# Two parts of the activations as one moving operand, and blocks of 256 columns

## The chip, the core and the metric

The kernel runs on one core of a Trainium2 chip. What counts is the device time of one execution in microseconds, as the median of the runs.

## What is computed

One decoder block for 256 tokens of width 2048, all in float32:

```python
h = rmsnorm(x, norm_w)
proj = h @ w_in          # z | x, B, C | dt | q | k | v | g_attn | g_merge
y = ssd_scan(silu(causal_dwconv(xBC)), softplus(dt + dt_bias), A)   # 64 heads in 8 groups
y_ssm = group_rmsnorm((y + D_skip * xs) * silu(z)) @ w_ssm_proj
y_attn = (attention(q, k, v) * silu(g_attn)) @ w_attn_proj          # 16 heads, causal
mixed = sigmoid(g_ssm + b) * y_ssm + sigmoid(g_att + b) * y_attn
out = rmsnorm(x + mixed @ w_out, final_norm_w)
```

With 256 tokens and blocks of 256, the block-sparse attention is plain causal attention of one block. The products with `w_in`, `w_ssm_proj`, `w_attn_proj` and `w_out` are nearly all of the work.

## The kernel before, in words

**Precision.** Each weight and each activation of the large products is split into an upper part and the rest (`hi`, `lo`), both of type float32r. A product is made of three matmuls: upper weights by upper activations, upper by lower, and lower by upper.

**The stream.** `stream()` (L46) lists blocks of weight columns in the order in which they are multiplied; a block is usually 512 columns wide with all 2048 rows, `sp` blocks have 1024 rows, `bc` blocks 256 columns. `chunks()` (L94) cuts each block into chunks of 128 partitions by 1024 values (512 KB), 480 in all; a chunk of a 512-column block holds two k tiles of 128 rows. The order is two `z` blocks, then eight groups of `bc`, `x`, `z` for the SSD branch (with gates `gs` and the projections `sp` between them), then `q`, `k`, `v`, `ga` four times for the attention, gates `gt` and projections `ap`, and `wo` at the end.

**The weight pipeline.** The loop over chunks stands at L801. In turn n it issues the load of chunk n + PF (L218; six buffers of `raw`, so a load waits until the chunk six before it is split), the upper part of chunk n + 4 on ScalarE (`split_hi`, L230; five buffers), the lower part of chunk n + 3 on VectorE (`split_lo`, L237; four buffers), one step of the tasks that take finished blocks out of PSUM (`evac`), the matmuls of chunk n, and a step of the SSD and attention tasks. These tasks are generators: each `yield` ends a step, and so the order of the instructions on each engine is written out by hand.

**The matmuls.** `matmuls` (L252, the instruction at L263) has two forms. Blocks `v` and `wo` have the activations as the stationary operand and 512 weight columns moving. All others, here called by-channel, have a strip of 128 weight columns stationary and the 256 tokens moving: three matmuls of 256 columns for each k tile and strip, into one of the four strips of an accumulator of 4 KB (two banks); there are two accumulators, `acc`, and four further banks for the small products. In the first two blocks the activations are those of `hp_hi`, `hp_lo`, not yet normalised; in `sp` and `ap` blocks they are named `ahi`, `alo` in the trace, elsewhere `h_hi`, `h_lo`.

**What follows a block.** `z_task`, `gate_task`, `sp_task`, `qkv_task`, `ap_task` read the whole accumulator once, on ScalarE or VectorE. `bc_task` and `x_task` make the causal convolution straight from PSUM, three VectorE operations to a step (L455). `ssd_task` does one group of the scan: transposes `px`, decays `e` (L524, L527, L531), products `yp` (L542), norm `pn`, and the two parts of the result for the `sp` blocks. Before block 15 a step of it is taken in every turn, later only in turns without an evacuation step, unless tasks pile up.

Of the kernel before, what the change touches and what calls it, by code (L numbers as in the profile page):

```python
# [24 lines left out]
# Chunks that loads and splits run ahead of the products.  # L25
PF, LA = 8, 3
# [19 lines left out]
def stream():  # L46
    """The weight stream: blocks (name, index, matrix, column pieces, first row, contraction rows)."""
# [4 lines left out]

    def sp(part, j):
        out.append(("sp", (part, j), "w_ssm_proj", [(j * 512, 512)], part * QR, QR))

    def gate(name, j):
        proj(name, j, ((C_GS if name == "gs" else C_GT) + j * 512, 512))

    for g in (0, 1):
        proj("z", g, (C_Z + g * 512, 512))  # L60
    for g in range(NG):
        proj("bc", g, (C_B + g * P, P), (C_C + g * P, P))
        proj("x", g, (C_X + g * 512, 512))
        if 1 < g + 1 < NG:
            proj("z", g + 1, (C_Z + (g + 1) * 512, 512))
        if g + 1 == NG:
            gate("gs", 0)
        if g > 2:
            part, half = divmod(g - 3, 2)
            sp(part, 2 * half)  # L70
            sp(part, 2 * half + 1)
# [9 lines left out]
    for u in range(4):  # L81
        for n, c in (("q", C_Q), ("k", C_K), ("v", C_V), ("ga", C_GA)):
            proj(n, u, (c + u * 512, 512))
    for j0 in (0, 2):
        for j in (j0, j0 + 1):
            gate("gt", j)
        for j in (j0, j0 + 1):
            out.append(("ap", j, "w_attn_proj", [(j * 512, 512)], 0, D))
# [5 lines left out]
def chunks():  # L94
    """(block number, first k tile, k tiles, columns) of each chunk of the stream."""
    out = []
    for b, (_, _, _, pieces, _, rows) in enumerate(stream()):
        cols = sum(n for _, n in pieces)
        per = CH // cols
        out += [(b, k, per, cols) for k in range(0, rows // P, per)]  # L100
    return out
# [16 lines left out]
def hybrid_block(  # L118
# [23 lines left out]
    def big(name, tag, dtype=F32):  # L142
        """4 KB of each partition; the tags are shared by what is not alive at the same time."""
# [36 lines left out]
    # The tensor engine's clock comes up while the first loads are under way.  # L180
# [3 lines left out]
    # mask[s, l]: s tile 0 against l 0..255, then s tile 1 against l 128..255.  # L184
# [7 lines left out]
    # amask[q, k]: q tile 0 against k 0..127, then q tile 1 against k 0..255.  # L192
# [11 lines left out]
    h_hi = hpool.tile([P, KT, S], F32R, name="h_hi")  # L204
    h_lo = hpool.tile([P, KT, S], F32R, name="h_lo")

# [1 line left out]
    raws, his, los = {}, {}, {}  # L208

    def halves(n):  # L210
        """The first chunk goes in two pieces, for an early start."""
        return (slice(0, CH),) if n else (slice(0, CH // 2), slice(CH // 2, CH))

    def load(n):
        if n < NCK:
            raws[n] = wpool.tile([P, CH], F32, tag="raw", name="raw", bufs=6)
            for h in halves(n):
                nc.sync.dma_start(raws[n][:, h], wpk[n][:, h])  # L218

    def part(n, which, bufs):  # L220
        """A part of chunk n; the last block's first half lies apart, as that block is gone through twice."""
        if NCK - 8 <= n < NCK - 4:
            return apool.tile([P, CH], F32R, tag="a" + which, name="a" + which)
        return wpool.tile([P, CH], F32R, tag="w" + which, name="w" + which, bufs=bufs)

    def split_hi(n):
        if n < NCK:
            his[n] = part(n, "hi", LA + 2)
# [3 lines left out]
    def split_lo(n):  # L232
        if n < NCK:
            los[n] = part(n, "lo", LA + 1)
# [5 lines left out]
    xt, hp_hi, hp_lo = [], [], []  # L240
    y_hi, y_lo = {}, {}
    o_hi, o_lo = {}, {}
    m_hi, m_lo = {}, {}

    def operand(name, k, sl=slice(0, S)):
        """(hi, lo) of k tile k of what the block multiplies."""
        for of, hi, lo in (("first", hp_hi, hp_lo), ("sp", y_hi, y_lo), ("ap", o_hi, o_lo), ("wo", m_hi, m_lo)):
            if name == of:
                return hi[k // 4][:, k % 4, sl], lo[k // 4][:, k % 4, sl]
        return h_hi[:, k, sl], h_lo[:, k, sl]  # L250

    def matmuls(n, acc, spans=((0, 0, 512), (1, 0, 512)), keep=False):  # L252
        b, k0, per, ncol = cks[n]
        name, i, _, _, row, rows = blocks[b]
        name = "first" if b < 2 else name
        last_k = rows // P - 1
        wh = his[n].rearrange("p (k c) -> p k c", k=per)
        wl = los[n].rearrange("p (k c) -> p k c", k=per)
        if not keep:
            del his[n], los[n]  # L260

        def mm(dst, a, bb, start, stop):
            nc.tensor.matmul(dst, a, bb, start=start, stop=stop, skip_group_check=True)  # L263

        if name in ("v", "wo"):
            for t, c0, c1 in spans:
                at = 0 if keep else t * 512
                dst = acc[:, at : at + c1 - c0]
                for i in range(per):
                    k = k0 + i  # L270
                    ah, al = operand(name, row // P + k, slice(t * P, (t + 1) * P))
                    mm(dst, ah, wh[:, i, c0:c1], k == 0, False)
                    mm(dst, ah, wl[:, i, c0:c1], False, False)
                    mm(dst, al, wh[:, i, c0:c1], False, k == last_k)
        else:
            for i in range(per):
                k = k0 + i
                ah, al = operand(name, row // P + k)
                for c in range(ncol // P):
                    dst = acc[:, c * S : (c + 1) * S]  # L280
                    cs = slice(c * P, (c + 1) * P)
                    mm(dst, wh[:, i, cs], ah, k == 0 and c % 2 == 0, False)
                    mm(dst, wh[:, i, cs], al, False, False)
                    mm(dst, wl[:, i, cs], ah, False, k == last_k)

# [1 line left out]
    for i in range(4):  # L287
        xt.append(big("xt", "xs" if i < 2 else "cumb"))
        hp_hi.append(apool.tile([P, 4, S], F32R, tag="ahi", name="hp_hi"))
        hp_lo.append(apool.tile([P, 4, S], F32R, tag="alo", name="hp_lo"))  # L290
    mpool = ctx.enter_context(tc.tile_pool(name="mpool", bufs=1))
    for n in range(8):
        ks = slice(n % 2 * 2, n % 2 * 2 + 2)
        nc.sync.dma_start(xt[n // 2][:, ks], xT[:, 2 * n : 2 * n + 2])
        if n < 6:
# [3 lines left out]
    for n in range(6, PF):  # L299
# [4 lines left out]
    def first_hi(n):  # L304
        if n < 8:
            for k in (2 * n, 2 * n + 1):
                nc.scalar.activation(
                    hp_hi[k // 4][:, k % 4], xt[k // 4][:, k % 4], AF.Identity, scale=nw[:, k : k + 1]
# [13 lines left out]
    def first_lo(n):  # L322
        if n < 8:
            for k in (2 * n, 2 * n + 1):
                nc.vector.scalar_tensor_tensor(
                    hp_lo[k // 4][:, k % 4], xt[k // 4][:, k % 4], nw[:, k : k + 1],
                    hp_hi[k // 4][:, k % 4].bitcast(F32), op0=OP.mult, op1=OP.subtract,
# [6 lines left out]
    def init_task():  # L334
        """The norm's factor of each token, along the free axis; h = h' * factor in its two parts."""
# [14 lines left out]
        for i in range(4):  # L350
# [6 lines left out]
            nc.scalar.copy(h_hi[:, ks], xt[i])  # L357
            yield
            nc.vector.tensor_sub(h_lo[:, ks], xt[i], h_hi[:, ks].bitcast(F32))
# [13 lines left out]
    def step(queue, heads=None):  # L373
        """One step of the first tasks of a queue; whether there was one."""
# [10 lines left out]
    scratch = dpool.tile([HEADS, S], F32, name="scratch")  # L385

    def dt_task(pd):
# [10 lines left out]
        # The two halves of the sum over k, transposed and added.  # L398
# [11 lines left out]
        # softplus(t) = max(t, 0) + log1p(exp(-|t|)); log1p(e) = 2 atanh(e / (2 + e))  # L410
# [35 lines left out]
    def tap(dst, u, ct):  # L446
        """Causal depthwise conv over the tokens (free axis): the token itself, then those before it."""
        nc.scalar.activation(dst, u, AF.Identity, bias=cb[:, ct : ct + 1], scale=cw[:, ct, 3:4])  # L448

    def conv(jobs):  # L450
        """The other taps of tiles (dst, u, ct), two tiles in turn, three operations a step."""
        ops = [(i + j, d) for i in range(0, len(jobs), 2) for d in (1, 2, 3) for j in range(2)]
        for at, (i, d) in enumerate(ops):
# [3 lines left out]
            )  # L457
            if at % 3 == 2:
                yield

    def bc_task(g, acc):
        bc = pool.tile([P, 2, S], F32, tag="bc", name="bc")
        jobs = [(bc[:, i], acc[:, i * S : (i + 1) * S], 32 + 8 * i + g) for i in range(2)]
# [14 lines left out]
    def x_task(g, acc):  # L478
        xs = big("xs", "xs")
        jobs = [(xs[:, i], acc[:, i * S : (i + 1) * S], 4 * g + i) for i in range(4)]  # L480
# [3 lines left out]
        ssd.append(ssd_task(g, xs))  # L484

    def ssd_task(g, xs):
# [118 lines left out]
        hi = apool.tile([P, 4, S], F32R, tag="ahi", name="ahi")  # L605
        lo = apool.tile([P, 4, S], F32R, tag="alo", name="alo")
        nc.scalar.copy(hi, y)
        yield
        nc.vector.tensor_sub(lo, y, hi.bitcast(F32))  # L609
        y_hi[g], y_lo[g] = hi, lo  # L610

# [1 line left out]
    SC = 128.0 ** -0.5  # L613

    def head_task(u, h, q, k, v, og):
# [30 lines left out]
        # k tile 0 against q 0..255, then k tile 1 against q 128..255  # L646
# [6 lines left out]
        if h == 3:  # L653
            yield
            hi = apool.tile([P, 4, S], F32R, tag="ahi", name="ahi")
            lo = apool.tile([P, 4, S], F32R, tag="alo", name="alo")
            nc.scalar.copy(hi, og)
            yield
            nc.vector.tensor_sub(lo, og, hi.bitcast(F32))
            o_hi[u], o_lo[u] = hi, lo  # L660

# [4 lines left out]
    def z_task(g, acc):  # L666
        t = big("z", "z")
        if g < 2:
            while "rsb" not in wk:
                yield  # L670
            nc.vector.tensor_tensor(
                t, acc.rearrange("p (a b) -> p a b", a=4),
                rsb.rearrange("p (o b) -> p o b", o=1).broadcast_to([P, 4, S]), op=OP.mult,
            )
            nc.scalar.activation(t, t, AF.Silu)
# [214 lines left out]
```

## Time and profile before

| | us |
|---|---|
| median of 3 runs (1467.83 to 1468.21) | 1467.96 |
| span of the profiled execution | 1466.1 |
| TensorE busy | 1454.4 (99%) |
| VectorE busy | 894.6 (61%) |
| ScalarE busy | 744.8 (51%) |
| mean DMA rate | 184 GB/s |

TensorE's row of busy time counts matmuls that overlap one another: the end of each is modelled, so the distance from one start to the next tells more than the length of one. Of the waits of the other engines, those for TensorE are time in which they had nothing to do.

### The profile page before, as it was taken

How to read it: one execution, taken by the hardware profiler on the slowest of the kernel's cores; microseconds unless marked ns; L12 is line 12 of the kernel's file. 1: busy time of each engine (PE TensorE's matmuls, PEld its weight loads, DVE VectorE, ACT ScalarE, POOL GpSimd, SP SyncE). 2: the span in 40 equal slices, each digit the busy share in tenths (PEclk: the TensorE clock that was granted, in tenths of full speed). 3: DMA queues.
4: the chain of work that ended last, by engine and by line, in shares of the span. 5: the costliest groups of instructions: out<-in, count | busy, mean ns of one | idle time of the engine just before them, and what ended most of it. 6: DMA issues, size and time to landing. Idle time of an engine off the chain costs nothing.

```text
span 1466.1 us, 27149 instructions
## 1 busy us (share of the span) xinstructions
PE 1454.4 (99%) x11410; PEld 1409.0 (96%) x11410; DVE 894.6 (61%) x1215; ACT 744.8 (51%) x870; POOL 5.3 (0%) x15
## 2 busy tenths in 40 slices
PE   9999999999999999999999999999999999999997
PEld 8999999999999999999999989999899999999886
DVE  7778777675667676866645455455454554545564
ACT  7545747564654565564544345445454454444452
POOL 0000000000000000000000000000000000000000
PEclk9999999999999999999999999999999999999999
DMA  8555656565565665665666565555655655666762
GB/s 326 164 170 190 206 163 202 158 208 180 176 191 179 181 193 163 198 209 165 177 184 186 180 187 166 176 173 165 192 160 173 187 158 175 185 185 177 267 211 80
DMA packets 74923, 269.99 MB, mean 184 GB/s; under 512 B 8304, under 2 KB 8624, under 8 KB 74416
## 3 DMA queue, kind: packets, MB, share of 16 engines
q1 hardware_dynamic: 74224, 267.49, 59.2%
q8 instruction: 89, 1.46, 0.4%
q10 hardware_dynamic: 576, 0.77, 0.2%
q14 instruction: 34, 0.28, 0.1%
HBM read 266.06 MB, written 2.16 MB: 183 GB/s over the span
## 4 chain that ended last, share of the span: by engine, by line
PE 98%; ACT 1%; DMA 0%; DVE 0%; issue 0%; SPq 0%; DVEq 0%
PE acc L263 93%; PE yp L542 2%; PE half L263 1%; PE px L502 0%; PE po L647 0%; PE ps L621 0%; DMA raw<-wpk 0%; PE pp L639 0%; PE pd L362 0%; PE ps L620 0%; PE po L648 0%; PE pcb L471 0%; PE pn L595 0%; ACT whi L230 0%; PE pcb L472 0%; ACT L684 0%
## 5 line engine op out<-in xcount | busy, mean ns | idle before, releaser
L237 DVE TENSOR_TENSOR wlo<-raw,whi 128x1024 fp32r<-128x1024 f32 (+1 forms) x477 | 582.2, 1222 | 492.2 <-PE acc L263 382.3
L230 ACT CAST whi<-raw 128x1024 fp32r<-128x1024 f32 (+1 forms) x477 | 497.4, 1048 | 559.9 <-PE acc L263 488.4
L263 PE MATMUL acc<-h_hi,whi 128*128 128x256 f32 x2432 | 697.0, 287 | 0.0
L263 PE MATMUL acc<-h_hi,wlo 128*128 128x256 f32 x2432 | 688.0, 283 | 0.0
L263 PE MATMUL acc<-h_lo,whi 128*128 128x256 f32 x2432 | 688.0, 283 | 0.0
L263 PEld LDWEIGHTS acc<-h_hi,whi 128*128 128x128 f32 x2432 | 466.3, 192 | 3.8 <-issue 3.0
L263 PEld LDWEIGHTS acc<-h_lo,whi 128*128 128x128 f32 x2432 | 466.6, 192 | 0.7
L263 PEld LDWEIGHTS acc<-h_hi,wlo 128*128 128x128 f32 x2432 | 466.3, 192 | 0.0
L263 PE MATMUL acc<-ahi,whi 128*128 128x256 f32 x768 | 218.7, 285 | 0.0
L263 PE MATMUL acc<-alo,whi 128*128 128x256 f32 x768 | 217.4, 283 | 0.2 <-DVE alo L609 0.2
L263 PE MATMUL acc<-ahi,wlo 128*128 128x256 f32 x768 | 217.3, 283 | 0.0
L263 PEld LDWEIGHTS acc<-ahi,whi 128*128 128x128 f32 x768 | 147.3, 192 | 0.9 <-issue 0.9
L263 PEld LDWEIGHTS acc<-alo,whi 128*128 128x128 f32 x768 | 147.4, 192 | 0.5 <-DVE alo L609 0.4
L263 PEld LDWEIGHTS acc<-ahi,wlo 128*128 128x128 f32 x768 | 147.4, 192 | 0.0
L263 PE MATMUL acc<-whi,h_hi 128*128 128x512 f32 x128 | 49.8, 389 | 0.0
L263 PE MATMUL acc<-wlo,h_hi 128*128 128x512 f32 x128 | 49.8, 389 | 0.0
L527 ACT ACTIVATE e<-e 128x768 f32<-128x768 f32 x32 | 27.1, 847 | 44.7 <-DVE e L524 44.6
L263 PE MATMUL acc<-whi,h_lo 128*128 128x512 f32 x128 | 49.8, 389 | 0.0
L455 DVE SCALAR_TENSOR_TENSOR xs<-acc,colt,xs 128x255 f32<-128x255 f32 (+2 forms) x96 | 40.2, 476 | 13.3 <-ACT xs L448 13.3
L263 PE MATMUL acc<-wlo,m_hi 128*128 128x512 f32 x104 | 40.6, 390 | 0.0
L263 PE MATMUL acc<-whi,m_lo 128*128 128x512 f32 x104 | 40.5, 389 | 0.0
L263 PE MATMUL acc<-whi,m_hi 128*128 128x512 f32 x104 | 40.5, 389 | 0.0
(191 smaller groups left out, 1091.9 us busy)
## 6 DMA issues: line engine op xcount, KB each, us to landing
raw<-wpk SPq DMA_DIRECT2D x479, 512.0 KB, 3.6
cumb<-scratch SPq DMA_DIRECT2D x16, 512.0 KB, 6.3
xt<-xT SPq DMA_DIRECT2D x8, 256.0 KB, 7.3
xr<-x SPq DMA_DIRECT2D x1, 2048.0 KB, 7.7
out<-xr SPq DMA_DIRECT2D x6, 256.0 KB, 2.9
fwt<-fw SPq DMA_DIRECT2D x1, 1024.0 KB, 9.7
raw<-wpk SPq DMA_DIRECT2D x2, 256.0 KB, 5.8
wd<-wdt SPq DMA_DIRECT2D x1, 512.0 KB, 9.2
```

The costliest lines, as they stand in the source:

```text
L230: nc.scalar.copy(his[n][:, h], raws[n][:, h])
L237: nc.vector.tensor_sub(los[n][:, h], r[:, h], his[n].bitcast(F32)[:, h])
L263: nc.tensor.matmul(dst, a, bb, start=start, stop=stop, skip_group_check=True)
L455: nc.vector.scalar_tensor_tensor(dst[:, d:], u[:, : S - d], cw[:, ct, 3 - d : 4 - d], dst[:, d:], op0=OP.mult, op1=OP.add)
L527: nc.scalar.activation(e, e, AF.Exp, scale=-1.0)
L542: nc.tensor.matmul(yp[r, st * P :], xd[:, st, h * 64 : (h + 1) * 64], e[:, j, :S] if st == 0 else e[:, j, S:384], start=(st == 0 and p % 2 ...
```

## The change

In the by-channel blocks the two parts of the activations lie side by side (`h2`, `hp`, `y2`, `o2`, each k tile 2 x 256 values). One matmul of 512 columns multiplies the upper weights with both, into one whole bank; a second of 256 columns multiplies the lower weights with the upper part and adds to the bank's second half. A strip of 128 weight columns thus takes a whole bank instead of half of one, and an accumulator holds 256 weight columns: most blocks are cut in halves of 256 columns (a chunk then holds four k tiles), the first `z` block stays 512 wide and takes both accumulators. `fold` adds the bank's two halves when a block leaves PSUM: a ScalarE copy of the lower sum, and a VectorE add of the upper one. The convolutions read the folded copy `u` in SBUF. The buffers of `raw` go from six to five and PF from eight to seven; the condition for a step of the SSD task now looks for a convolution step only. Blocks `v` and `wo` are computed as before (`by_token`).

```diff
-PF, LA = 8, 3
+PF, LA = 7, 3
+RAW = 5
@@ stream
+    def halves(name, i, c):
+        for half in range(2):
+            proj(name, (i, half), (c + half * 256, 256))
     def sp(part, j):
-        out.append(("sp", (part, j), "w_ssm_proj", [(j * 512, 512)], part * QR, QR))
+        for half in range(2):
+            out.append(("sp", (part, j, half), "w_ssm_proj", [(j * 512 + half * 256, 256)], part * QR, QR))
-    for g in (0, 1):
-        proj("z", g, (C_Z + g * 512, 512))
+    proj("z", (0, 2), (C_Z, 512))
+    halves("z", 1, C_Z + 512)
...
@@ matmuls
-            for i in range(per):
-                k = k0 + i
-                ah, al = operand(name, row // P + k)
-                for c in range(ncol // P):
-                    dst = acc[:, c * S : (c + 1) * S]
-                    cs = slice(c * P, (c + 1) * P)
-                    mm(dst, wh[:, i, cs], ah, k == 0 and c % 2 == 0, False)
-                    mm(dst, wh[:, i, cs], al, False, False)
-                    mm(dst, wl[:, i, cs], ah, False, k == last_k)
+    def by_channel(n, accs):
...
+        order = [(i, c) for i in range(per) for c in range(ncol // P)]
+        if len(accs) > 1 and k0 + per > last_k:
+            order.sort(key=lambda ic: ic[1])
+        for i, c in order:
+            k = k0 + i
+            a = operand(name, row // P + k)
+            dst = accs[c // 2].rearrange("p (c s) -> p c s", c=2)[:, c % 2]
+            cs = slice(c * P, (c + 1) * P)
+            mm(dst, wh[:, i, cs], a.rearrange("p a s -> p (a s)"), k == 0, False)
+            mm(dst[:, S:], wl[:, i, cs], a[:, 0], False, k == last_k)
+
+    def sums(acc):
+        a = acc.rearrange("p (c h s) -> p h c s", c=2, h=2)
+        return a[:, 0], a[:, 1]
+
+    def fold(dst, acc):
+        upper, lower = sums(acc)
+        nc.scalar.copy(dst, lower)
+        nc.vector.tensor_add(dst, upper, dst)
@@ start
-        if n < 6:
+        if n < RAW:
             load(n)
...
-    for n in range(6, PF):
+    for n in range(RAW, PF):
         load(n)
@@ x_task
+        u = pool.tile([P, 2, S], F32, tag="u", name="u", bufs=2)
+        fold(u, acc)
+        yield
+        jobs = [(xs[:, 2 * half + i], u[:, i], 4 * g + 2 * half + i) for i in range(2)]
@@ sp_task
         if part == 0:
-            nc.scalar.copy(m, acc)
+            fold(m, acc)
         else:
-            nc.vector.tensor_add(m, acc, m)
+            for a in sums(acc):
+                nc.vector.tensor_add(m, a, m)
@@ the stream
-        if not busy or b < 15 or len(ssd) > 1 or n > last_x - 8:
+        if not wk["busy"] or n < 96 or len(ssd) > 1 or n > last_x - 8:
             step(ssd, 1)
```

## Rows read from the trace of the kernel before

**Rows 1.** The page, its first part: busy time and instructions of each engine.
```profile
PE 1454.4 (99%) x11410; PEld 1409.0 (96%) x11410; DVE 894.6 (61%) x1215; ACT 744.8 (51%) x870; POOL 5.3 (0%) x15
```

**Rows 2.** Span and mean granted TensorE clock of the core.
```profile
core 0: 1466.1 us, clock 0.999
```

**Rows 3.** The page, the chain that ended last, its shares by engine.
```profile
PE 98%; ACT 1%; DMA 0%; DVE 0%; issue 0%; SPq 0%; DVEq 0%
```

**Rows 4.** Groups by shape, TensorE: count, busy us, mean ns, idle before, releaser.
```profile
L263 PE MATMUL acc<-h_hi,whi 128*128 128x256 f32 x2432 | 697.0, 287 | 0.0
...
L263 PE MATMUL acc<-ahi,whi 128*128 128x256 f32 x768 | 218.7, 285 | 0.0
...
L263 PE MATMUL acc<-whi,h_hi 128*128 128x512 f32 x128 | 49.8, 389 | 0.0
...
L263 PE MATMUL acc<-hp_hi,whi 128*128 128x256 f32 x128 | 36.8, 288 | 1.2 <-ACT whi L230 1.2
L263 PE MATMUL acc<-hp_hi,wlo 128*128 128x256 f32 x128 | 36.4, 284 | 1.0 <-DVE wlo L237 1.0
```

**Rows 5.** Order of time, TensorE, 840 to 864 us: start us, length us.
```profile
839.79 0.28 PE L263 MATMUL acc<-h_lo,whi 128*128 128x256 f32 x1
...
842.07 0.28 PE L263 MATMUL acc<-h_hi,wlo 128*128 128x256 f32 x1
842.19 0.40 PE L263 MATMUL acc<-whi,h_hi 128*128 128x512 f32 x1
...
844.03 0.39 PE L263 MATMUL acc<-whi,h_lo 128*128 128x512 f32 x1
...
863.75 0.39 PE L263 MATMUL acc<-whi,h_lo 128*128 128x512 f32 x1
863.98 0.28 PE L263 MATMUL acc<-h_hi,whi 128*128 128x256 f32 x1
```

**Rows 6.** Who waited for whom: us in total, times, longest us.
```profile
ACT whi L230 <- PE acc L263: 488.4, 283, 3.5
DVE wlo L237 <- PE acc L263: 382.3, 245, 3.7
...
DVE ar L844 <- ACT ar L842: 18.5, 8, 3.8
...
ACT whi L230 <- DMA raw<-wpk: 6.6, 5, 2.9
```

**Rows 7.** Groups by shape, weight loads.
```profile
L263 PEld LDWEIGHTS acc<-h_hi,whi 128*128 128x128 f32 x2432 | 466.3, 192 | 3.8 <-issue 3.0
```

**Rows 8.** Groups by shape, VectorE: additions that read PSUM.
```profile
L696 DVE TENSOR_TENSOR mix<-acc,mix 128x1024 f32<-128x1024 f32 x12 | 14.6, 1218 | 0.0
...
L736 DVE TENSOR_TENSOR xr<-acc,xr 128x512 f32<-128x512 f32 x7 | 4.8, 686 | 7.5 <-PE acc L263 7.5
```

**Rows 9.** Groups by shape, ScalarE: copies out of PSUM.
```profile
L642 ACT COPY p<-pp 128x384 f32<-128x384 f32 x16 | 7.6, 474 | 0.0
...
L694 ACT COPY mix<-acc 128x1024 f32<-128x1024 f32 x4 | 4.0, 1004 | 0.0
```

**Rows 10.** Stretch of one SSD group: us, busy of PE, PEld, DVE, ACT, POOL.
```profile
129.20:192.00 62.80, 62.80 (x528) 61.53 (x526) 47.81 (x78) 37.97 (x43) 0.00 (x0) 1.00 0.60 184
```

**Rows 11.** Order of time, VectorE, one SSD group.
```profile
134.93 0.95 DVE L531 TENSOR_TENSOR e<-e,cbm 128x768 f32<-128x768 f32 x1
...
138.67 1.26 DVE L455 SCALAR_TENSOR_TENSOR xs<-acc,colt,xs 128x255 f32<-128x255 f32 x3 [1.55 <-ACT xs L448]
```

**Rows 12.** Order of time, TensorE, the same place.
```profile
138.60 1.52 PE L542 MATMUL yp<-e,xd 128*64 128x256 f32 x16
```

**Rows 13.** Order of time, VectorE and ScalarE, where the second block starts.
```profile
32.48 1.23 DVE L237 TENSOR_TENSOR wlo<-raw,whi 128x1024 fp32r<-128x1024 f32 x1 [0.29 <-issue]
...
32.30 1.05 ACT L230 CAST whi<-raw 128x1024 fp32r<-128x1024 f32 x1 [1.66 <-PE acc L263]
```

**Rows 14.** DMA issues: count, KB each, median us to landing.
```profile
raw<-wpk SPq DMA_DIRECT2D x479, 512.0 KB, 3.6
```

## What the change is expected to do

> **What bounds the kernel now.** I read the page from its top. TensorE is busy for 99% of the span [rows 1], at a mean granted clock of 0.999, the 2.4 GHz level [rows 2], and the chain that ended last is TensorE for 98% [rows 3]. But busy time of pipelined matmuls says little: in the groups by shape a 256-column matmul lasts 283 to 288 ns and there are 3 x 3328 = 9984 of them in the three orders of the by-channel blocks, together more than the span holds [rows 4]. So the next view is the one in order of time, and there starts are what counts. From 839.79 to 842.07 us stand 19 steps between 256-column matmuls, 120.0 ns each; from 844.03 to 863.75 us stand 87 steps between 512-column ones, 226.7 ns each [rows 5]. The 256 columns between the two cost 106.7 ns, one column per cycle of 2.4 GHz, and so 13.3 ns are left for each matmul, whatever its width. The other engines wait for TensorE, not it for them: VectorE for 382.3 us and ScalarE for 488.4 us at the two weight splits [rows 6].
>
> **Part 1, three matmuls become two.** For each k tile and 128-column strip of a by-channel block the kernel issues upper weights by upper activations, upper by lower, lower by upper: 3 x 120.0 = 360.0 ns. The change issues one matmul of 512 columns and one of 256. The columns are the same 768; one of three fixed parts goes. That is 226.7 + 120.0 = 346.7 ns, 13.3 ns less. The mixed order is shown too: the 256-column matmul at 842.07 is followed 0.12 us later by a 512-column one, and the 512-column one at 863.75 is followed 0.23 us later by a 256-column one [rows 5]; the width of the earlier one sets the step, in both directions. There are 2432 + 768 + 128 = 3328 triples [rows 4]; blocks v and wo keep their form. 3328 x 13.33 ns = 44.4 us, all of it on the path that sets the end, as TensorE waits for nothing there. The weight load lasts 192 ns [rows 7] and starts one matmul ahead; under a 512-column matmul it has more cover than now, under the 256-column one the same as now. The small matmuls (`px`, `yp`, `pcb`, `pn`, attention) keep their number.
>
> The Trainium skill speaks against this sum: "TensorE: Matmul & The Clock Gate", section Back-to-back issue gap, gives N / 2.4 + 2.5 ns at full clock, a fixed part of 2.5 ns instead of 13.3. By that, the sum of this part would be 3328 x 2.5 = 8.3 us, an estimate from the page. The trace disagrees: by that rule the steps would be 109 and 216 ns, and they are 120.0 and 226.7 [rows 5].
>
> **Part 2, folding on ScalarE and VectorE.** Each 256-column block now leaves PSUM as two sums. 96 blocks are folded by a ScalarE copy of 128x512 and a VectorE add of the same shape; 24 `sp` blocks by two adds. The add from PSUM at 128x512 took 686 ns [rows 8]. The copy lies between 474 ns at 384 elements and 1004 ns at 1024 [rows 9]; on the line between them 512 cost 580 ns. VectorE: 96 x 0.69 = 66 us, `sp` 48 x 0.69 against 12 x 1.218 = +18 us, `ap` smaller pieces +2 us: 895 to some 981 us. ScalarE: 96 x 0.58 = 56 us, less the copies of `q`, `k` and the first `sp` part (12 x 1.0): 745 to some 789 us. Both stay far below the new span, but a mean hides the stage that is tightest. That is a group of the SSD stage, 20 chunks in 62.8 us, in which VectorE is busy 47.81 us and ScalarE 37.97 [rows 10]. After: 480 matmuls x 0.12 = 57.6 become 160 x 0.3467 = 55.5 us, the group 60.7 us; five folds make VectorE 47.8 + 5 x 0.69 = 51.3 (84%) and ScalarE 40.9 (67%). So it is covered on average. The cover is the wait for TensorE that the splits have now [rows 6].
>
> What the cover may miss is one step: the fold's add stands on VectorE in order behind a copy that stands on ScalarE behind a cast of 1.05 us, and what is queued behind the add is the SSD step of that chunk, for which TensorE's `yp` matmuls wait. Now the decay product before `yp` ends at 134.93 + 0.95 = 135.88 [rows 11] and `yp` starts at 138.60 [rows 12]: 2.7 us to spare. The convolution now runs a chunk later than before (fold first), onto the decay steps, in the chunks before 96 where both run in every chunk: 1.26 us of it in one chunk, three instructions [rows 11], 0.69 of fold, some 0.4 of waiting for the copy and 0.1 of a shorter chunk, 2.4 us in all. So the margin shrinks to about 0.3 us and will be missed now and then. From below: nothing. From above: all 16 `yp` steps of eight groups miss by 0.6 us, 10 us. I take 2.5 us, 8 steps of the early groups at 0.3, nearer to the lower end since later groups hold their step back while a convolution runs.
>
> **Part 3, the accumulators.** The first z block keeps 512 columns and takes both accumulators, so the block behind it waits for its first fold. At that place the first block ends at about 32.2 us and the next starts at 32.46; ScalarE's cast starts at 32.30 and VectorE's split at 32.48 [rows 13], and both stand ahead of the fold. Cast 1.05 (to 33.35), copy 0.58 (33.95 with the handover), add 0.69 (34.65): TensorE starts at 34.7 instead of 32.46, less what it would wait anyway, +2.3, call it 2.4 us. The lower end is 1.3 us, copy and add alone, if the cast goes first. Elsewhere a block of four chunks gives the fold 11.1 us and a `sp` block of two chunks 5.5 us; split 1.2 and two adds 1.4 end 2.6 us behind the block: hidden, with 2.9 us for a backlog.
>
> **Part 4, loads.** Five raw buffers for six, seven chunks ahead for eight. A load waits until its buffer is split and lands 3.6 us after issue [rows 14]. Now five chunks (14.4 us) less the split (1.5 us) and the landing stand between: 9.3 us to spare; after, four of 2.77 us: 11.1 - 5.1 = 6.0 us. ScalarE waits for a load for 6.6 us in all, five times [rows 6], so this is free in the steady state. At the start the sixth chunk's load goes behind three more pieces of `xt` and `wd` on SP's queue: I put 0.5 us for it (0 to 2). The start has 1.2 and 1.0 us of TensorE waits [rows 4], and at best the new order takes these away, 2 us below nothing.
>
> **The sum.** 1466.1 - 44.4 + 2.4 + 0.5 + 2.5 = 1427.1 us of span. The median of the runs, 1467.96, is 1.9 us above the profiled span, which the start and end around it add: 1429.0 us. Ends: 1466.1 - 44.4 + 1.3 - 2 + 1.9 = 1422.9 and 1466.1 - 44.4 + 2.4 + 2 + 10 + 1.9 = 1438.0.
>
> **Rivals.** (a) VectorE becomes the bound, and the kernel ends slower. Place: the SSD groups; mechanism: each fold stops VectorE until ScalarE's copy is there. Price: VectorE's waits for ScalarE at `ar`, where a short chain crosses the engines, were 18.5 us in 8 waits, 2.3 us each and 3.8 at most [rows 6]. At 2.3 us a fold the group needs 51.3 + 11.5 = 62.8 us on VectorE, 2.1 more than TensorE; eight groups 17 us and 1466.1 - 44.4 + 2.9 + 17 + 1.9 = 1443.5 us: most of the gain stays. At 3.8 us it needs 70.3, 9.6 over, 77 us, and the time is 1503.5. It decides from 3.0 us a fold (5.5 us over in each of eight groups). For it: both queues run in order. Against it: ScalarE is idle at most chunk ends [rows 6], so the copy is done 1.7 us and VectorE's own split 1.2 us behind the chunk, a wait of 0.5. (b) The fixed part does not go: the pair's 512 columns cost as much as two matmuls (the instruction split again, or the time bound to columns). Saving 0 and 2.9 us to pay: 1466.1 + 2.9 + 1.9 = 1470.9 us. Against it: the steps of v at 226.7 in the same kernel and precision. (c) Only a small part of the 13.3 ns goes with the number of matmuls, the rest stays with the strip and its two weight loads, which remain: with a fifth, 2.7 ns, 3328 x 2.7 = 8.9 us saved, 1466.1 - 8.9 + 2.9 + 1.9 = 1462.0 us. The two mixed steps of [rows 5] speak against it. The figure of the Trainium skill in part 1 ("TensorE: Matmul & The Clock Gate") would come out beside this, at 8.3 us saved; no other number hangs on it.
>
> **How the numbers follow.** Forecast, 1422.9 to 1438: 0.82. Rival (a) mild, around 1443.5: 0.09; full, slower: 0.04. (b) 0.03, (c) 0.02. The range is the forecast's with its ends and the first of mild (a): 1422 to 1440. Measured to about 0.2%, faster is 0.82 + 0.09 + 0.02 = 0.93, no change 0.03 (b), slower 0.04.
>
> **What would show it.** In the profile after: 3328 matmuls of 128x512 against `whi` and as many of 128x256 against `wlo`; a step of 0.227 behind the first and 0.120 behind the second, alternating; 128 x 512 copies and adds at 0.58 and 0.69 us; VectorE near 981, ScalarE near 789 us; one TensorE gap of about 2 us near 32 us. Wrong are: a step of 0.24 behind the wide matmul (rival b); idle TensorE at `yp` or at block starts beyond 10 us in all (rival a), with VectorE over 90% in the slices of the first 250 us; a wait for `raw` in the steady state (part 4).

## The result, and the profile after

The changed kernel takes 1451.99 us (median of four runs, 1451.23 to 1452.76) against 1467.95 us: ratio 0.9892, 95% interval 0.9878 to 0.9906. It is 16.0 us faster; the forecast was 39 us, and the time lies 12 us above the range.

The page of the changed kernel, its totals and the shares of its chain of waits, answering to [rows 1, 3]:

```profile
span 1449.5 us, 20757 instructions
PE 1431.0 (99%) x8082; PEld 1229.7 (85%) x8082; DVE 976.3 (67%) x1363; ACT 786.7 (54%) x962; POOL 3.8 (0%) x15
PE 96%; DVE 2%; ACT 1%; DMA 0%; issue 0%; DVEq 0%; SPq 0%; ACTq 0%
```

TensorE still sets the end. VectorE and ScalarE grew to 976.3 and 786.7 us, where 981 and 789 were forecast. The groups by line, operation and shape (total us, mean ns of one, then idle time before them and what ended it), answering to [rows 4]:

```profile
L281 PE MATMUL acc<-h,whi 128*128 128x512 f32 x2432 | 869.8, 401 | 0.0
L281 PE MATMUL acc<-h,wlo 128*128 128x256 f32 x2432 | 681.9, 280 | 0.0
...
L281 PE MATMUL acc<-hp,whi 128*128 128x512 f32 x128 | 46.9, 409 | 3.4 <-DVE z L326 1.9 <-ACT whi L246 1.5
...
L594 PE MATMUL yp<-e,xd 128*64 128x256 f32 x128 | 20.2, 394 | 4.7 <-DVE e L583 4.7
```

The 9984 matmuls of [rows 4] have become 3328 wide and 3328 narrow ones, as written. TensorE's idle time is 9.4 us (3.4, 4.7, and 1.3 in other groups) against 3.5 before. The rest of the time is in the steps. In order of time (start, duration in us), answering to [rows 5]:

```profile
745.14 0.40 PE L281 MATMUL acc<-h,whi 128*128 128x512 f32 x1
745.37 0.28 PE L281 MATMUL acc<-h,wlo 128*128 128x256 f32 x1
745.49 0.40 PE L281 MATMUL acc<-h,whi 128*128 128x512 f32 x1
745.73 0.28 PE L281 MATMUL acc<-h,wlo 128*128 128x256 f32 x1
745.85 0.40 PE L281 MATMUL acc<-h,whi 128*128 128x512 f32 x1
746.08 0.28 PE L281 MATMUL acc<-h,wlo 128*128 128x256 f32 x1
746.20 0.40 PE L281 MATMUL acc<-h,whi 128*128 128x512 f32 x1
...
798.85 0.40 PE L281 MATMUL acc<-h,whi 128*128 128x512 f32 x1
...
810.15 0.40 PE L281 MATMUL acc<-h,whi 128*128 128x512 f32 x1
```

Three pairs take 746.20 - 745.14 = 1.06 us, 353.3 ns each; 32 pairs of one block of q take 11.30 us, 353.1 ns each. Forecast were 346.7. Read to the nanosecond, the steps behind the three wide matmuls are 232, 240 and 236 ns (226.7 was expected) and behind the narrow ones 118, 120 and 114. But a part of the kernel does run at the forecast:

```profile
191.51 0.39 PE L281 MATMUL acc<-h,whi 128*128 128x512 f32 x1
...
198.44 0.39 PE L281 MATMUL acc<-h,whi 128*128 128x512 f32 x1
```

20 pairs take 6.93 us, 346.5 ns each. Other matmuls (the small ones, and those of `v`) cut the pairs into 105 stretches, and each stretch, behind its first few pairs, keeps one of two rhythms: in this trace 20 stretches with 592 pairs have 346.7 ns, 85 with 2736 pairs have 353.3 (counted from the starts of all matmuls). So the steps save 592 x 13.3 + 2736 x 6.7 = 26.1 us, and the idle time takes back 9.4 - 3.5 = 5.9: 1466.1 - 26.1 + 5.9 = 1445.9 us of span, and 1449.5 were measured. Some 1.7 of the missing 3.6 us are a lower clock at the start (length, busy us of TensorE, weight loads, VectorE, ScalarE and GpSimd, clock, DMA share, GB/s):

```profile
0.00:20.00 20.00, 17.16 (x82) 15.15 (x83) 12.40 (x22) 14.15 (x25) 2.49 (x12) 0.91 0.87 315
```

The mean of 0.91 comes from a stretch at the 1.2 GHz level between 9 and 13 us, behind 4 us in which TensorE was busy for 2.27; the kernel before has 1.00 in its first 20 us. The rest lies in the small matmuls (0.8 us) and behind the start of the last one (0.9 us).

The waits of the changed kernel (us in total, times, longest), answering to [rows 6]:

```profile
ACT whi L246 <- PE acc L281: 335.7, 195, 3.4
DVE wlo L253 <- PE acc L281: 277.1, 208, 2.6
DVE u L326 <- ACT u L325: 16.5, 28, 2.7
DVE z L326 <- ACT z L325: 14.1, 15, 2.0
ACT whi L246 <- DMA raw<-wpk: 10.9, 6, 4.7
DVE mix L326 <- ACT mix L325: 8.9, 7, 1.7
```

Nearly all folds wait for ScalarE (lines with L325), but briefly; with the smaller groups `sig`, `q`, `k` and `ga` it is some 49 us in 90 of 96 folds, 0.5 us each. The splits' waits for TensorE still cover that.

### The profile page after: what moved, and what is told of

It is laid out like the page before. It is cut to its first block, busy times and chain, and to the rows that moved or that the text cites. A ratio compares the mean times of both kernels' runs of the same rounds, so it can differ in the third digit from the quotient of the medians.

```text
span 1449.5 us, 20757 instructions
## 1 busy us (share of the span) xinstructions
PE 1431.0 (99%) x8082; PEld 1229.7 (85%) x8082; DVE 976.3 (67%) x1363; ACT 786.7 (54%) x962; POOL 3.8 (0%) x15
## 4 chain that ended last, share of the span: by engine, by line
PE 96%; DVE 2%; ACT 1%; DMA 0%; issue 0%; DVEq 0%; SPq 0%; ACTq 0%
PE acc L281 91%; PE yp L594 1%; PE half L281 1%; PE px L554 0%; PE ps L672 0%; PE po L698 0%; DMA raw<-wpk 0%; ACT whi L246 0%; PE pp L690 0%; DVE wlo L253 0%; PE pd L403 0%; DVE e L583 0%; DVE xs L496 0%; PE po L699 0%; PE ps L671 0%; PE pn L647 0%
## 5 line engine op out<-in xcount | busy, mean ns | idle before, releaser
L281 PE MATMUL acc<-h,whi 128*128 128x512 f32 x2432 | 869.8, 401 | 0.0
L281 PE MATMUL acc<-h,wlo 128*128 128x256 f32 x2432 | 681.9, 280 | 0.0
L281 PEld LDWEIGHTS acc<-h,whi 128*128 128x128 f32 x2432 | 456.9, 188 | 111.4 <-issue 2.4
L281 PEld LDWEIGHTS acc<-h,wlo 128*128 128x128 f32 x2432 | 459.2, 189 | 0.7
L281 PE MATMUL acc<-y,whi 128*128 128x512 f32 x512 | 182.7, 400 | 0.0
L281 PE MATMUL acc<-y,wlo 128*128 128x256 f32 x512 | 143.6, 280 | 0.0
L281 PEld LDWEIGHTS acc<-y,whi 128*128 128x128 f32 x512 | 96.2, 188 | 23.9 <-issue 0.9
L281 PEld LDWEIGHTS acc<-y,wlo 128*128 128x128 f32 x512 | 96.7, 189 | 0.0
L281 PE MATMUL acc<-o,whi 128*128 128x512 f32 x256 | 90.5, 399 | 0.0
L281 PE MATMUL acc<-whi,h 128*128 128x512 f32 x256 | 79.6, 389 | 0.0
```

## The experiments

The expectations number the theories for the 6.6 ns that most pairs are longer. Theory 1: alternating widths cost this in any case. Theories 2 and 3 look for it in where the narrow matmul writes and in what it reads. Theory 4: traffic of the other engines. Theories 5 and 6 came after the first series: the bank that is written, and the point at which a series starts. The kernel before took 1468.08 us beside most of these runs and 1467.97 beside the last kernels.

**Matmuls alone.** Of the kernel only sixteen series are left, 96 turns each, with no other engine at work, in one execution; `wide` is the 512-column and `slim` the 256-column matmul. Three of them:

```diff
+    pattern("cmix", loop(W, lambda t, i: slim(t, 0, i)))
+    pattern("dbank", loop(W, lambda t, i: slim(t, 1, i)))
+    pattern("elow", loop(W, lambda t, i: slim(t, 0, i, at=0)))
```

> Leaves the whole decoder block out: it loads one weight chunk and a piece of x, and runs sixteen series of matmuls with nothing beside them, then writes the banks out. In the changed kernel the steady step is 232 to 241 ns behind a 512-column matmul that a 256-column one follows, and 113 to 120 ns behind that one, 353.3 ns for the pair, where v's 512 columns take 226.7 and the kernel before's 256 columns 120.0. Theory 1, the change of width costs: alone on the engine the pair takes 353 ns too, in the same bank (cmix), in another bank (dbank), in the bank's lower half (elow), with another moving tile (fsrc) and with the same weights (gsamew); two wide and two narrow in turn take 700 for four (hpairs), eight and eight 347.5 per pair (ieights). Theory 2, the second matmul adds to the half bank that the first has just written: cmix 353, but dbank and elow 347. Theory 3, the moving tile is read twice in a row, or the weights come from two tiles: fsrc or gsamew 347. Theory 4, ScalarE's and VectorE's traffic beside it: all of them 347.

In order of time, the first and last wide matmuls of a stretch of `cmix` and of `elow`:

```profile
89.70 0.39 PE L168 MATMUL cmix<-hh,wh 128*128 128x512 f32 x1
89.93 0.28 PE L174 MATMUL cmix<-hh,wl 128*128 128x256 f32 x1
90.04 0.39 PE L168 MATMUL cmix<-hh,wh 128*128 128x512 f32 x1
...
108.07 0.39 PE L168 MATMUL cmix<-hh,wh 128*128 128x512 f32 x1
149.66 0.40 PE L168 MATMUL elow<-hh,wh 128*128 128x512 f32 x1
149.90 0.28 PE L174 MATMUL elow<-hh,wl 128*128 128x256 f32 x1
...
176.87 0.40 PE L168 MATMUL elow<-hh,wh 128*128 128x512 f32 x1
```

`cmix`, the very order of the changed kernel, runs 53 pairs in 18.37 us, 346.6 ns each; `elow` 77 pairs in 27.21 us, 353.4 each. One width alone gives 226.7 (512 columns), 173.3 (384), 120.0 (256) and 111.7 (128). Another bank, other moving data or the same weights leave 346.7; two wide and two narrow by turns give 348.3 a pair, eight and eight 349.2; one wide and two narrow 466.7, which is their sum; 512 with 384 columns 413.3 where the sum is 400.0. (All means here and below are taken over whole turns.) So theory 1 falls as it was put, since some alternations cost nothing; theory 4 can't be the whole cause, since `elow` has the kernel's 353 with no other engine at work. Nothing here speaks for theories 2 and 3, and `elow` pointed to the place written to.

**Eight wide, then eight narrow.** All wide matmuls of a chunk go first (where a block has two accumulators, of each half):

```diff
-        for i, c in order:
...
-            mm(dst, wh[:, i, cs], a.rearrange("p a s -> p (a s)"), k == 0, False)
-            mm(dst[:, S:], wl[:, i, cs], a[:, 0], False, k == last_k)
...
+            for i, c in order[at : at + half]:
+                wide(i, c)
+            for i, c in order[at : at + half]:
+                slim(i, c)
```

> The changed kernel with all 512-column matmuls of a chunk first and then all 256-column ones (in the first block by accumulator). Theory 1 (the change of width costs 6.6 ns a pair): one change in eight pairs stays, 3328 x 6.6 x 7/8 = 19 us less than the changed kernel's 1452.0, so 1433. Theory 2 (the half bank just written): the same half bank comes eight matmuls later, 22 us less, 1430. Theory 4 (other engines' traffic): 1452.

1441.41 us, ratio 0.9817 (0.98 to 0.9833), 10.6 us below the changed kernel. One chunk in order of time:

```profile
746.57 2.00 PE L281 MATMUL acc<-h,whi 128*128 128x512 f32 x8
748.41 1.12 PE L281 MATMUL acc<-h,wlo 128*128 128x256 f32 x8
749.37 2.00 PE L281 MATMUL acc<-h,whi 128*128 128x512 f32 x8
```

Eight pairs take 2.80 us, 350 ns each, in most chunks 349.2: more than half of the excess is gone, with the same matmuls. Behind the change of width the first wide steps are 234, 236, 228, 232 and 231 ns, and only then 227; the first narrow one is 114, the next ones 119 and 120. The excess lies in the five steps after a change of width and not in one, so theory 1's 1433 was missed too: a change and back costs 8 x 2.5 = 20 ns instead of 6.6. It is the 349.2 of the eights without other engines: theory 4 is out. The time fits the two rhythms: 2736 pairs gain 4.2 ns and 592 lose 2.5, which is 9.9 us.

**The narrow one a pair later**, so that it doesn't follow the wide one whose sum it continues:

```diff
-            mm(dst[:, S:], wl[:, i, cs], a[:, 0], False, k == last_k)
...
+            if at:
+                slim(*order[at - 1])
...
```

> The changed kernel with the widths still in turn, but each 256-column matmul one place later, behind the wide one of the next strip, so that it adds to another bank than the one just written. Theory 1 (change of width): nothing changes, 1452. Theory 2 (the half bank just written): 22 us less, 1430.

1448.34 us, ratio 0.9864 (0.985 to 0.9879); in the middle of a chunk the same 353 ns. Theory 1's 1452 is much nearer than theory 2's 1430: that the narrow matmul adds to the half bank just written is not what costs. Of the 3.7 us that this kernel is below the changed one, some 1.7 go with the clock: in its first 20 us it has 1.00 and not 0.91.

**Everything but the wide matmul.** The changed kernel with three matmuls of 256 columns again; accumulators, folds and loads stay as changed:

```diff
-            mm(dst, wh[:, i, cs], a.rearrange("p a s -> p (a s)"), k == 0, False)
+            mm(dst[:, :S], wh[:, i, cs], a[:, 0], k == 0, False)
+            mm(dst[:, S:], wh[:, i, cs], a[:, 1], False, False)
...
```

> The changed kernel with the wide matmul cut in two again: three matmuls of 256 columns as before, all the rest (halved blocks, folds, the wide first block, five raw buffers) as changed. It prices the rest alone. By the steady steps it is 3328 x (360.0 - 353.3) = 22 us slower than the changed kernel, 1474, some 6 us over the kernel before; had the pair brought the forecast 44.4 us and the rest cost 28, it would be 1496.

1475.44 us, ratio 1.0047 (1.0032 to 1.0062). So parts 2 to 4 cost 7.4 us, and the wide matmul brings 1475.44 - 1451.99 = 23.4. Busy time by stretches of TensorE in this kernel (length, busy us, count, granted clock, DMA share, GB/s):

```profile
34.00:35.00 1.00, 0.00 (x0) 1.00 1.04 246
...
36.00:37.00 1.00, 1.00 (x8) 0.50 0.77 291
...
40.00:41.00 1.00, 1.00 (x11) 1.00 0.03 12
```

Behind the wait for the first fold, the clock stands at 0.50, the 1.2 GHz level, from about 36.0 to 39.4 us, and a triple takes 0.64 us instead of 0.36. That costs 3.4 / 2 = 1.7 us. The profiled execution of the changed kernel has the same wait, but its stretch behind it is at 1.00, the 2.4 GHz level (length, then busy us of TensorE, weight loads, VectorE, ScalarE and GpSimd, clock, DMA share, GB/s):

```profile
35.00:40.00 5.00, 5.00 (x30) 4.33 (x29) 1.81 (x3) 2.30 (x3) 0.00 (x0) 1.00 0.50 186
```

If that holds for all executions of both, the wide matmul brings 21.7 rather than 23.4 us; the steps in two rhythms say 26.1. That it holds isn't shown: the four executions of the kernel with three matmuls have mean clocks of 0.996 to 0.998, and these don't order their times. In the first 20 us this kernel has 0.91 like the changed one, another 1.7 us that the kernel before doesn't have. So in its profiled execution 3.4 of the 7.7 us of span above the kernel before are lower clock; its waits of TensorE are 8.3 us instead of 3.5, 4.8 more.

**Banks, with the matmuls alone and in the kernel.** Sixteen further series vary bank, half and start; and the changed kernel with the chunk's pairs always sorted by bank:

```diff
+    pattern("same", pairs([(0, 1)]))
+    pattern("turn", pairs([(0, 1), (1, 3)]))
...
+    pattern("low", pairs([(0, 0)]))
...
+    pattern("samew2", pairs([(0, 1)], 2))
```

> Leaves the whole decoder block out; series of 96 pairs (512 columns, then 256) alone on TensorE, as in the first such run, where one accumulator bank and its upper half took 346.7 ns a pair and the lower half 353.3. Theory 5, the banks that the output goes to decide: same and otherhalf 346.7; turn, the order of the changed kernel (bank 0, its upper half, bank 1, its upper half), 353.3 as there; fours and twos (four or two pairs to a bank) between, 348 and 350; low and turnlow 353.3; the same with one or two 256-column matmuls ahead (w1, w2). Theory 6, the engine falls into one of two rhythms by the phase at the start: the w1 and w2 series differ from their twins, and turn can be 346.7. alt512, 512 columns to two banks in turn: 226.7 under either (the steps settle within six matmuls in the series of eight).

```diff
         if len(accs) > 1 and k0 + per > last_k:
             order.sort(key=lambda ic: ic[1])
+        order.sort(key=lambda ic: ic[1])
```

> The changed kernel with the loops over the four k tiles and the two strips of a chunk exchanged: four pairs to one bank, then four to the other. Theory 5 (the bank decides): most pairs at 346.7, one change of bank in four pairs, 3328 x 6.6 x 3/4 = 16 us less than 1452.0, 1436. Theory 1 (the change of width) and theory 6 (rhythm by phase): 1452.

`same` is `cmix` under another name, at another place of the program. In order of time:

```profile
59.70 0.40 PE L168 MATMUL same<-hh,wh 128*128 128x512 f32 x1
59.94 0.28 PE L174 MATMUL same<-hh,wl 128*128 128x256 f32 x1
...
86.91 0.40 PE L168 MATMUL same<-hh,wh 128*128 128x512 f32 x1
```

77 pairs take 27.21 us, 353.4 each, where `cmix` had 346.6; `low`, which is `elow`, now has 346.7. The finding of the first series turns round, so it was not the place written to. Of the others `turnlow` and `samew2` ran at 346.7, and all the rest of this order at 353.3. That `samew2` (two narrow matmuls ahead) and `loww1` (one ahead) run unlike `same` and `low` is what theory 6 expects, but they also stand elsewhere in the program. Sorted by bank the kernel takes 1451.93 us, ratio 0.9892 (0.9877 to 0.9907), no change. Theory 5 falls in both.

**Starts, groups and other widths, again alone:**

```diff
+    for w in range(3, 9):
+        pattern("ph" + "abcdef"[w - 3], pairs([(0, 1)], w))
...
+    pattern("snkeight", groups(8, True))
...
+    pattern("wb", widths(512, 448))
+    pattern("wc", widths(384, 256))
```

> Leaves the whole decoder block out; series of matmuls alone on TensorE. Theory 6 (two rhythms, chosen by the phase at the start): the same series of 96 pairs (512, 256) behind three to eight single 256-column matmuls runs at 346.7 in some and at 353.3 in others, each for its whole length. If the rhythm is chosen by what the series is, all six are alike. Groups of equal width pay for a change of width, not for each pair: groups of four 351 to 352 a pair, of sixteen 348; of eight with every second group turned round (half as many changes) 348.3, of two turned round 348 to 350. Two widths in turn other than these (512/320, 512/448, 384/256, 448/256, 320/256): if the loss belongs to any alternation, 6 to 13 ns over the sum of columns at 2.4 GHz and 13.3 ns each; if it belongs to 256 columns that barely cover the next weight load, 512/320 and 512/448 have none.

Behind three to eight single narrow matmuls all six series run at 353.3: nothing for theory 6 here. But it isn't out: in the changed kernel, too, a stretch has one rhythm from its start to the next interruption. Groups of four give 350.8 a pair, of sixteen 347.9; eights by turns from either side (wide, narrow, narrow, wide), where the widths change as often as in sixteens, 347.9 as well. Pairs of 512 with 320 columns take 380.0 (the sum of their single steps is 373.3, with 13.3 ns and one column per cycle of 2.4 GHz for the widths not run alone), 512 with 448 take 437.8 (426.7), but 384, 448 or 320 with 256 take 293.3, 320.0 and 266.7, which is their sum. Among these widths the excess comes only where one of the two has 512 columns.

**The first series once more**, unchanged, as another execution of the same program, on another chip.

> Leaves the whole decoder block out; the first set of series once more, unchanged. If the rhythm belongs to the program (its instructions and their order), cmix, dbank, fsrc, gsamew and pmix run at 346.7 ns a pair again and elow at 353.3. If it belongs to the execution (the phase in which the engine happens to meet a series), they change places.

Every series of two widths has the same mean step as before to 0.01 ns (`cmix` again 346.7 a pair, `elow` 353.4). Only the first series, of 512 columns alone, differs, since it begins with more steps of 427 ns. The rhythm belongs to the program, not to the execution.

**The copy a step ahead of the add.** In `bc_task` and `x_task` the fold is cut in two:

```diff
-        fold(u, acc)
+        upper, lower = sums(acc)
+        nc.scalar.copy(u, lower)
+        yield
+        nc.vector.tensor_add(u, upper, u)
```

> The changed kernel with the fold of bc and x blocks spread over two steps: ScalarE's copy in one turn, VectorE's addition in the next, the convolution one turn later. If the three waits of yp (1.65 to 1.9 us past the step) come from VectorE standing 2.7 us at the addition for the copy, they go: 1452.0 - 5 = 1447. If they come from the sum of VectorE's work in these turns (the convolution on the decay steps), they stay or move: 1451 to 1453.

1449.26 us, ratio 0.9871 (0.9857 to 0.9886), 2.7 us below the changed kernel. Waits of TensorE in this kernel (us in total, times, longest):

```profile
PE yp L600 <- DVE e L589: 1.5, 3, 0.6
```

It was 4.7 us. About two thirds of the `yp` waits come from the add that stands behind the copy; 1.5 us remain. The 2.7 us are net of another loss: in the profiled execution the clock behind the first fold is 0.66 from 35 to 40 us, where the changed kernel has 1.00.

**The kernel before with five raw buffers**, seven chunks ahead:

```diff
-PF, LA = 8, 3
+PF, LA = 7, 3
...
-            raws[n] = wpool.tile([P, CH], F32, tag="raw", name="raw", bufs=6)
+            raws[n] = wpool.tile([P, CH], F32, tag="raw", name="raw", bufs=5)
...
```

> The kernel before with five raw buffers and seven chunks ahead, nothing else. The prediction's part 4: free in the steady state, 0 to 2 us at the start, 1468.0 to 1470. If a later load is waited for in each group, 1475 and more.

1468.41 us, ratio 1.0002 (0.9993 to 1.0012): free.

**Better than both.** Grouped, with the fold cut in two, and in turn 8 the evacuation step ahead of the splits, so that the first block's fold isn't queued behind them; then also every second chunk with its narrow matmuls first:

```diff
+        if n == 8:
+            step(evac)
...
+            forms = (wide, slim) if k0 // per % 2 == 0 or len(accs) > 1 else (slim, wide)
+            for f in forms:
+                for i, c in order[at : at + half]:
+                    f(i, c)
```

> The changed kernel with three edits: a chunk's wide matmuls first, then its narrow ones; the fold of bc and x spread over two turns; in the turn behind the first z block the evacuation ahead of the splits. The steps at 349.5 give 3328 x 3.8 = 12.6 us (measured alone: 10.6), the fold 2.7 us, the first evacuation 1.5 to 2.5 us: 1452.0 - 15.5 = 1436.5.

> The same, with every second chunk of a block taking its narrow matmuls first, so that the widths change once in sixteen matmuls instead of twice. If the change of width is what costs (some 9 ns for each of the 300 changes saved, and less where it falls on a block's end), 2 to 4 us less than without it: 1433.5. If the loss were tied to the number of pairs, no difference: 1436.5.

1435.63 us, ratio 0.9779 (0.9762 to 0.9795), and 1433.64 us, 0.9765 (0.975 to 0.9779): 34.3 us below the kernel before, 18.4 below the changed one. The last in order of time:

```profile
740.43 3.82 PE L281 MATMUL acc<-h,whi 128*128 128x512 f32 x16
744.08 2.08 PE L281 MATMUL acc<-h,wlo 128*128 128x256 f32 x16
745.99 0.40 PE L281 MATMUL acc<-h,whi 128*128 128x512 f32 x1
```

Sixteen pairs take 5.56 us, 347.5 ns each, over whole turns 347.9. Against the 349.2 of the grouped order that is 1.2 ns for each of 3328 pairs, 4.1 us; 2.0 were measured, but the waits are 1.1 us longer here, and the clock of the first 20 us is 0.91 instead of 1.00. The waits of TensorE in it:

```profile
PE yp L610 <- DVE e L599: 2.2, 3, 0.8
...
PE acc L281 <- DVE z L336: 0.2, 1, 0.2
```

The wait for the first fold has gone from 1.9 to 0.2 us; in the kernel without the turned chunks it is 1.1.

## Why the prediction was too low

**Part 1, the term that was mis-sized.** Forecast 44.4 us, measured 23.4 by the kernel with three matmuls and 26.1 by the steps. The failed step is the sentence on the mixed order, that the width of the earlier matmul sets the step in both directions. The step behind a wide matmul was read at 863.75, at the end of a long series, and the steady one was counted from 844.03. The kernel before shows the change of width at 842.19 itself [rows 5], and behind it:

```profile
842.42 0.40 PE L263 MATMUL acc<-wlo,h_hi 128*128 128x512 f32 x1
842.66 0.39 PE L263 MATMUL acc<-whi,h_lo 128*128 128x512 f32 x1
...
843.35 0.39 PE L263 MATMUL acc<-whi,h_lo 128*128 128x512 f32 x1
```

The first five wide steps take 843.35 - 842.19 = 1.16 us, where five of 226.7 ns are 1.13; to the nanosecond they are 234, 236, 228, 232 and 231, and only then 227, just as in the grouped kernel. So the trace before already had steps that the earlier width doesn't set, and the count began behind them. What an alternation loses it did not show: the first wide step, 234, and the first narrow one, 113, make 347, the forecast's pair. Only an alternation shows the two rhythms. Of the 13.3 ns a pair 6.7 stay in 2736 of the 3328 pairs, 18.2 of the 44.4 us, and the other 592 bring what was forecast. Why a stretch gets one rhythm or the other stays open.

**Which rival was near.** (b) is out: a wide matmul alone costs 226.7 ns and the three-matmul form 23.4 us more. Its sign, a step of 0.24 behind the wide matmul, nearly came true all the same (some 236 on average); it could not tell (b) from this, as the step behind the narrow one is shorter in turn (117). (c) came nearest in kind with "only a part goes", but more than half goes, not a fifth, and its mechanism is not what the runs show: pairs with as many weight loads run at 346.7, in `cmix` and in 592 places of the kernel, and other pairs of unequal widths cost exactly their sum. The formula of the Trainium skill cited in part 1 ("TensorE: Matmul & The Clock Gate", section Back-to-back issue gap), which that section gives for isolated matmuls and not for a stream with weight loads as here, gives an estimate of 109, 162.5 and 216 ns for 256, 384 and 512 columns; the series of one width measured 120.0, 173.3 and 226.7. There the measurement decides: the fixed part is 13.3 ns at these widths, as [rows 5] had it, though not at every width: 128 columns alone take 111.7 ns.

**Part 2.** VectorE and ScalarE came out within 1% of the forecast, copy and add at 0.58 and 0.69 us, 0.5 us of waiting a fold: rival (a) did not decide. The `yp` waits were taken at 2.5 us in eight small steps; they are 4.7 us in three large ones, within the bounds of 0 and 10, in the early groups as said. VectorE and ScalarE of the changed kernel ahead of the `yp` step at 201.4 us, in order of time:

```profile
192.12 0.69 DVE L326 TENSOR_TENSOR u<-acc,u 128x512 f32<-128x512 f32 x1 [2.72 <-ACT u L325]
...
194.73 1.27 DVE L496 SCALAR_TENSOR_TENSOR xs<-u,colt,xs 128x255 f32<-128x255 f32 x3
...
200.39 0.96 DVE L583 TENSOR_TENSOR e<-e,cbm 128x768 f32<-128x768 f32 x1
```

```profile
186.59 1.28 ACT L512 ACT_TABLE_LOAD   x1
...
188.53 1.28 ACT L579 ACT_TABLE_LOAD   x1
...
190.57 1.03 ACT L246 CAST whi<-raw 128x1024 fp32r<-128x1024 f32 x1
191.51 0.58 ACT L325 COPY u<-acc 128x512 f32<-128x512 f32 x1
```

VectorE stands 2.72 us at the fold's add; the copy it wants stands on ScalarE behind a cast, as the prediction had it, but also behind two table loads of 1.28 us each with their functions, which it had not counted. The convolution and the decay product then come late, and TensorE waits 1.65 us for that product.

**Part 3.** TensorE starts the next block at 34.70 us, forecast 34.7; the wait is 1.9 us. The order was as forecast too: cast, copies, adds. Not foreseen was that such a gap can be followed by a stretch at the lower clock: in the profiled executions of the kernel with three matmuls (1.7 us), of the grouped one (0.73 from 35 to 40 us) and of the one with the fold in two (0.66), but not in that of the changed kernel.

**Part 4.** Free in the steady state, as said: five buffers in the kernel before change nothing. ScalarE's waits for `raw` rose from 6.6 to 10.9 us, off the path.

**Together.** The changed kernel's idle time grew by 5.9 us, where parts 2 to 4 had forecast 5.4. That is close partly by luck, since the errors cancel: the `yp` waits cost 4.7 instead of 2.5, the first fold 1.9 instead of 2.4, and the start gave back 0.7 instead of costing 0.5. Of the 23.0 us between 1429.0 and 1452.0, 18.2 are the pairs at 353.3, 1.7 the lower clock in the first 20 us, 0.5 the idle time, and 0.6 the distance of the median from the profiled span (2.5 instead of 1.9). Most of the last 2.0 us is the 0.8 and 0.9 us in the small matmuls and at the end.

## What to carry to other kernels

Two steady series don't give the step of an alternation: read the steps right behind the change too, look for a stretch in the profile that alternates, or keep the bound open by the whole gain. Where matmuls of 512 columns and narrower ones must be mixed, issue them in groups of one width; here this gave 10.6 us for a reordering within each chunk. A fold shared by two engines should have a step between its halves, so that the second engine doesn't stand in order behind the first one's queue.

## What the runs showed of the hardware that was not expected

Alternating a 512-column matmul with one of 256 runs in one of two rhythms, 346.7 or 353.3 ns a pair, one for a whole series or a whole stretch of the kernel (20 stretches against 85). 512 with 320, 384 or 448 columns cost 6.7, 13.3 and 11.1 ns over the sum of their single steps, in one series each; 384, 448 or 320 with 256 cost nothing. In groups of eight and of sixteen a change of width and back costs 20 ns (8 x 2.5, 16 x 1.3), in fours 16, in twos 3. Which rhythm a series gets is fixed by the program: the same program gave it again on another chip, and the same order at another place of another program gave the other. None of these alone decides it: the bank, the half, the moving data, the weights, the traffic of other engines, as the same choice of all of them was seen in both rhythms. What selects it stays open; how a stretch starts is not excluded.
